# Attention and one output product of a hybrid encoder layer: fillers placed at the ends of heads, gate weights split in two halves, transposed x copied before it is cast

## The chip, the cores and the metric

The kernel runs on one core of a Trainium2 chip. The metric is the device time of one execution in microseconds (us). The engines are TensorE (PE in the profile, with its weight loads as PEld), VectorE (DVE), ScalarE (ACT), GpSimd (POOL) and SyncE (SP), which issues the transfers.

## The reference

One encoder layer on x of 1024 tokens by 1024 channels, in fp32:

```python
h = x @ w_in                                   # 1024 x 5120
qa, ka, va, qb, kb, vb, ga, gb = split(h)      # 6 x 512 columns, 2 x 1024
y_a = chunk_band_attention(qa, ka, va, rel_bias) @ w_proj_a
y_b = stick_breaking_attention(qb, kb, vb) @ w_proj_b
mix = (sigmoid(ga + b_a) * y_a + sigmoid(gb + b_b) * y_b) @ w_out
x = layer_norm(2 ** 0.25 * x + mix)
g, u = split(x @ w_ffn_in)                     # 2 x 2816 columns
x = layer_norm(2 ** 0.25 * x + (silu(g) * u) @ w_ffn_out)
```

Branch A has 8 heads of softmax attention over a band of 9 chunks of 64 keys, with a bias by relative distance. Branch B has 8 heads of stick-breaking attention: the weight of a key is sigmoid(z) times the product of 1 - sigmoid over the keys between it and the query, for all earlier keys.

## The kernel before, in words

**Precision.** A product in fp32 is made of three matmuls on rounded operands, high by high, high by low and low by high. `split` (L109 to L111) makes the two operands: ScalarE casts the high part (L110), VectorE subtracts it from the source (L111). Most large products use seven block products instead of eight, on sums of blocks.

**Stages.** The input projection takes the first 333 us of the profiled execution; the 16 heads of attention run from there to some 650 us; then the projection of branch B and the output product with w_out follow, to some 770; then the FFN's first product (L180) to 1160 and its second (L1496) to the end. The framework's scheduler orders the instructions of each engine from the order of the code and their dependences; some are pinned in the written order (`tc.keep_in_program_order`).

**Attention.** The loop around L1003 goes through 16 heads (`hidx` 0 to 7 are branch A, `br` 0; 8 to 15 are branch B), each in 12 steps (`pos`): 8 for the query group g = 0 and 4 for g = 1. A step contains

- the *weight units* that come due, by the table `LEAD` (L37): one unit makes the scores of 128 queries (L695, L696) and turns them into weights, for branch A in `soft_block` (L729: bias and minimum on VectorE at L738, exp on ScalarE at L744, division on POOL at L749), for branch B in `stick_block` (L763: two sigmoids on ScalarE at L776 and L777, a scan on VectorE at L779, a product on POOL at L784);
- `turn`: PE transposes weights (L807) into a bank "tr", and `split` makes the tile `pt` of it;
- `mult`: the products with the values (L820, L821) into the bank "pv", two steps later (`LAG`); the group's last one is followed by a ScalarE copy (L839) that empties the bank into `yt` or `yv`; a transfer moves one half to other partitions, and POOL adds it in (L843);
- *fillers*: independent matmuls, drawn from the generator `fill_all` (L856) by `fill_until(goal)` (L951). One filler is one 128x128 by 128x512 matmul: of a gate (`gate`, L591, matmuls at L598) or, later, of the projection of branch A (`yAps`). `FILL` (L39) is the number per head; `goal` rises by a twelfth of it in each step, half of it filled ahead of the step's product and half behind. All heads together have 480.

The weights of gates 11 to 15 are prepared while the gate before is in its second half: `begin_w` (L538) loads 128x1024, `end` casts the high part on ScalarE in one instruction (L549) and subtracts on POOL in one (L550).

PSUM has eight banks of 128x512 (L45): "mm" 2 for fillers, "sc" 2 for scores, "tr" 3 for transposes, "pv" 1. In branch B one "tr" bank holds an identity for the scan (`ident_ps`).

**The output product and x.** For token tiles 4 to 7 the product with w_out is made plainly, in two column halves `hf`, tile after tile (24 matmuls each at L117, L118 and L120, tiles `ops4_0` to `ops7_1`). Meanwhile the layer norm of tiles 0 to 3 ends. `x1_operands(0, ...)` (L1171) transposes them on PE (L1178), for each `kt` of 0 to 3 the column blocks kt and kt + 4 into one "tr" bank each (`x1ps0_0` to `x1ps0_7`, four transposes per bank). Out of a bank come a cast and a subtraction (`split`, tiles `x1A1`) and an unrounded copy on ScalarE (L1188, tile `x1raw`); the second call, `x1_operands(1, ...)`, does the same for tiles 4 to 7 with `x1low`. The first call comes once, in the second column half behind tile 4:

```python
            if hf == 1:
                norm_1(tt)
                if tt == 4:
                    x1_operands(0, acc_t)
        if hf == 0:
            left_f(2)
```

The functions that the change touches are these:

## Time and profile before

| | |
|---|---|
| runs shown | 1425.95 us median of 3 (1424.87 to 1426.73) |
| profiled execution | 1425.8 us |
| its span | 1424.0 us, 1.8 us less than its time |
| granted TensorE clock | 0.999 |
| attention, branch A, 333 to 455 us | busy in 122.0 us: PE 120.9, ACT 97.2, DVE 93.4, POOL 66.0 |
| attention, branch B, 455 to 650 us | busy in 195.0 us: PE 193.9, DVE 159.8, ACT 151.4, POOL 138.7 |
| the first call of x1_operands and its surroundings, 751 to 770 us | busy in 19.0 us: PE 18.1, DVE 17.1, ACT 8.4 |

A row of the timeline shows the start in us from the span's start, the duration, the engine, the line, the operation with its tiles (buffer numbers left out), the shapes and the number of like instructions in a row; in brackets stands how long the engine stood idle before it, and what released it. Matmuls are pipelined: a row's duration reaches into the next one's, so a PE that stands in short waits can still count as busy. The profile gives one execution, on the one core.

### The profile page before, as it was taken

What the parts mean: (1) busy time and instruction counts of PE and PEld (TensorE: products, weight loads), DVE (VectorE), ACT (ScalarE), POOL (GpSimd) and SP (SyncE); (2) the same over time, 40 slices, a digit from 0 to 9 for tenths busy, and PEclk for the clock granted to TensorE, in tenths of its full rate; (3) what the DMA queues carried; (4) which work ended last, traced back from release to release, by engine and by line L of the source; (5) the groups of instructions that cost most, each with busy time, mean ns of one, the idle gap of its engine ahead of it and who ended that gap; (6) DMA issues with size and microseconds to landing.
All of it is one profiled execution on the core that took longest, in us unless ns stands there. A gap on an engine that the chain in (4) does not pass through costs nothing.

```text
span 1424.0 us, 19039 instructions
## 1 busy us (share of the span) xinstructions
PE 1412.3 (99%) x6672; PEld 1172.8 (82%) x6672; DVE 1054.5 (74%) x1669; ACT 683.0 (48%) x1188; POOL 245.9 (17%) x313
## 2 busy tenths in 40 slices
PE   9999999999999999999999999999999999999997
PEld 7888888888888888888888888888888888888886
DVE  8866657635777778878988947776777656978767
ACT  6444444555778788774423624444444433212201
POOL 0000000002555779750001000000000000100014
PEclk9999999999999999999999999999999999999999
DMA  7486478856676468755651224443444458787602
GB/s 255 159 295 223 163 251 311 294 183 212 213 222 199 135 228 296 249 196 198 231 198 69 74 75 163 148 148 135 150 159 163 148 192 280 281 312 238 204 15 104
DMA packets 104974, 276.54 MB, mean 194 GB/s; under 512 B 10400, under 2 KB 26784, under 8 KB 104880
## 3 DMA queue, kind: packets, MB, share of 16 engines
q1 hardware_dynamic: 104880, 275.35, 55.9%
q8 instruction: 52, 0.85, 0.3%
q14 instruction: 42, 0.34, 0.1%
HBM read 179.33 MB, written 92.30 MB: 191 GB/s over the span
## 4 chain that ended last, share of the span: by engine, by line
PE 93%; DVE 4%; ACT 2%; issue 1%; DMA 0%; POOL 0%; DVEq 0%; ACTq 0%; SPq 0%
PE sxf L180 16%; PE sxp L180 9%; PE szf L180 8%; PE dx L1496 6%; PE v L482 5%; PE szp L180 5%; PE gps L598 4%; PE syf L180 4%; PE dz L1496 3%; PE yAps L896 3%; PE syp L180 2%; PE tp_b L807 2%; PE ops L1343 2%; PE tp_a L807 2%; PE plain L348 2%; PE fpswh_h L118 2%
## 5 line engine op out<-in xcount | busy, mean ns | idle before, releaser
L784 POOL TENSOR_TENSOR w_b<-w_b,kp_b 128x511 f32<-128x511 f32 (+3 forms) x96 | 96.1, 1017 | 24.9 <-DVE kp_b L779 17.1
L1452 POOL TENSOR_TENSOR wdyt<-wdyt 128x512 f32<-128x512 f32 x8 | 11.2, 1405 | 512.5 <-DVE wdgt L1451 492.0
L779 DVE TENSOR_TENSOR_SCAN kp_b<-kp_b,ident_ps 128x512 f32<-128x512 f32 (+2 forms) x64 | 56.5, 884 | 23.3 <-ACT kp_b L776 22.4
L776 ACT ACTIVATE kp_b<-sc_b 128x512 f32<-128x512 f32 (+3 forms) x96 | 48.4, 505 | 30.7 <-PE sc_b L696 27.4
L180 PE MATMUL szf<-x1S63h,wcf 128*128 128x512 f32 x168 | 55.1, 389 | 0.0
L111 DVE TENSOR_TENSOR pt_b<-tp_b,pt_b 128x512 fp32r<-128x512 f32 (+1 forms) x96 | 50.0, 544 | 6.9 <-ACT pt_b L110 6.3
L719 POOL MEMSET bias<- 64x64 f32 x2 | 0.3, 144 | 313.4 <-ACT bias L715 313.4
L1427 DVE TENSOR_TENSOR x<-dx,x 128x512 f32<-128x512 f32 x64 | 43.3, 685 | 14.7 <-PE dx L1496 14.6
L111 DVE TENSOR_TENSOR sl<-h,sl 128x512 fp32r<-128x512 f32 x56 | 38.3, 685 | 19.5 <-ACT sl L110 19.5
L749 POOL TENSOR_SCALAR w_a<-w_a,st_a 128x640 f32<-128x640 f32 (+2 forms) x64 | 42.3, 666 | 57.3 <-PE sc_a L696 23.8
L110 ACT CAST sl<-h 128x512 fp32r<-128x512 f32 x56 | 34.7, 619 | 35.3 <-PE syf L180 17.1
L110 ACT CAST pt_b<-tp_b 128x512 fp32r<-128x512 f32 (+1 forms) x96 | 47.5, 505 | 8.0 <-PE tp_b L807 7.6
L744 ACT ACTIVATE w_a<-w_a,st_a 128x640 f32<-128x640 f32 (+2 forms) x64 | 44.8, 702 | 13.5 <-DVE st_a L738 12.2
L1156 POOL TENSOR_TENSOR mv<-mv,neghalf 128x1 f32<-128x1 f32 x16 | 11.9, 744 | 222.1 <-DVE mv L1155 222.0
L1274 ACT ACTIVATE h<-sxf 128x512 f32<-128x512 f32 x21 | 12.5, 597 | 77.3 <-PE sxf L180 77.3
L777 ACT ACTIVATE w_b<-sc_b 128x511 f32<-128x511 f32 (+3 forms) x96 | 48.6, 506 | 0.0
L111 DVE TENSOR_TENSOR pt_a<-tp_a,pt_a 128x512 fp32r<-128x512 f32 (+1 forms) x96 | 44.9, 485 | 4.8 <-ACT pt_a L110 3.1
L807 PE MATMUL tp_b<-ident,w_b 128*128 128x128 f32 x288 | 47.8, 273 | 0.4 <-DVE pt_b L111 0.3
L110 ACT CAST pt_a<-tp_a 128x512 fp32r<-128x512 f32 (+1 forms) x96 | 39.1, 432 | 11.0 <-PE tp_a L807 10.8
L807 PE MATMUL tp_a<-ident,w_a 128*128 128x128 f32 x240 | 43.2, 275 | 1.0 <-POOL w_a L749 0.4
L807 PEld LDWEIGHTS tp_b<-ident,w_b 128*128 128x128 f32 x288 | 35.6, 140 | 9.6 <-PE sc_b L696 1.3
L598 PE MATMUL gps<-xl,wh_g 128*128 128x512 f32 x96 | 43.0, 448 | 0.0
(1787 smaller groups left out, 4814.3 us busy)
## 6 DMA issues: line engine op xcount, KB each, us to landing
s_dr<-sl SPq DMA_DIRECT2D x112, 256.0 KB, 2.3
sd<-s_dr SPq DMA_DIRECT2D x56, 512.0 KB, 4.7
wLf<-in_w_ffn_in_dram SPq DMA_DIRECT2D x22, 512.0 KB, 4.5
wRf<-in_w_ffn_in_dram SPq DMA_DIRECT2D x22, 512.0 KB, 3.6
v_dr<-vc SPq DMA_DIRECT2D x16, 512.0 KB, 3.2
qs<-q_dr SPq DMA_DIRECT2D x16, 512.0 KB, 6.9
kh<-k_dr SPq DMA_DIRECT2D x16, 512.0 KB, 6.1
kl<-k_dr SPq DMA_DIRECT2D x16, 512.0 KB, 6.9
```

What stands on the lines that cost most here:

```text
L110: return (nc.scalar.copy(dst_h, src), nc.vector.tensor_tensor(dst_l, src, dst_h.bitcast(F32), ALU.subtract))
L111: nc.vector.tensor_tensor(dst_l, src, dst_h.bitcast(F32), ALU.subtract))
L180: mm(acc, lw[:, ks], rx, start=(first and kt == i == 0), stop=(kt == 3 and i == 2), skip_group_check=not first)
L482: mm(accs[j], a, b, start=(first and kt == n == 0), stop=(kt == 3 and n == 2), skip_group_check=True)
L598: mm(acc[hf], lw[:, ks], rx[k][:, (LO, HI)[hf]], start=(k == j == 0), stop=(k == KT - 1 and j == 2))
L744: nc.scalar.activation(s[:, 0:w], s[:, 0:w], AF.Exp, bias=st[:, m:m + 1], scale=-1.0, accum_out=st[:, 2:3])
L776: nc.scalar.activation(kp[:, c0:e], sc[:, 0:n], AF.Sigmoid, scale=-1.0)
L777: nc.scalar.activation(be[:, m0:e], sc[:, m0 - c0:n], AF.Sigmoid)
L779: nc.vector.tensor_tensor_scan(kp[:, 0:e], kp[:, 0:e], ident_ps()[:, 0:e], 0.0, ALU.mult, ALU.add)
L784: nc.gpsimd.tensor_tensor(be[:, m0:e], be[:, m0:e], kp[:, m0 - 1:e - 1], ALU.mult)
L807: tr(tp[:, (qb - lo_q) * P:(qb - lo_q + 1) * P], wt[qb - q0][:, (kb - qb) * P:(kb - qb + 1) * P], ident)
L1496: mm(acc, a, b, start=(first and i == n == 0), stop=(i == n - 1 == 1), skip_group_check=not first)
```

## The change

There are three parts. Line numbers behind the first places shift by up to 22 in the changed kernel: L598 becomes L607, L695 L706, L749 L760, L807 L818, L820 L831, L1188 L1207.

**Fillers.** `FILL` of heads 8 to 11 goes from 40, 40, 39, 39 to 39, 39, 38, 38. In the loop, ahead of a step's weight units: in head 7 `goal` rises by 2 more at pos 3 and again at pos 4, and at pos 5 it falls by 1 (three more in all); in the other heads of branch A it rises by 1 at pos 3 and falls by 1 at pos 5. In branch A at pos 2 `fill_until(goal + 0.5)` is called ahead of the step's weight units, which at that step hold the first scores of the next head.

**Gate weights.** Inside `fill_all`, `end` casts and subtracts columns 0 to 511 where it did all 1024, and puts columns 512 to 1023 on the list `rest`; `gate` takes them from it behind the third of eight blocks of its second half, nine fillers later.

**Transposed x.** `x1_operands` copies each bank to SBUF first, and `split` reads the copy; this holds for both calls. The first call is made in three pieces: block 0 behind the whole first column half, blocks 1 and 2 behind tile 4 of the second, block 3 behind tile 5.

```diff
-FILL = (18, 18, 18, 18, 18, 18, 18, 34, 40, 40, 39, 39, 40, 38, 38, 38)
+FILL = (18, 18, 18, 18, 18, 18, 18, 34, 39, 39, 38, 38, 40, 38, 38, 38)
...
-        def end(tied=False):
+        def end(tied=False, rest=None):
             hi = hl(f"wh_{name}", F32R)
             lo = hl(f"wl_{name}", F32R)
-            for ins in (nc.scalar.copy(hi, r),
-                        lo_eng.tensor_tensor(lo, r, hi.bitcast(F32), ALU.subtract)):
-                if tied:
-                    tc.keep_in_program_order(ins)
+
+            def part(cs):
+                for ins in (nc.scalar.copy(hi[:, cs], r[:, cs]),
+                            lo_eng.tensor_tensor(lo[:, cs], r[:, cs], hi[:, cs].bitcast(F32),
+                                                 ALU.subtract)):
+                    if tied:
+                        tc.keep_in_program_order(ins)
+
+            if rest is None:
+                part(slice(0, 1024))
+            else:
+                part(LO)
+                rest.append(lambda: part(HI))
             return hi, lo
...
                 for k in range(KT):
                     yield from part(hf, k)
+                    if hf and k == 2 and rest:
+                        rest.pop()()
                 take(hf)
...
-            yield from gate(i, w, lambda: got.append(end(True)))
+            yield from gate(i, w, lambda: got.append(end(True, rest)))
...
+        if hidx == 7 and pos in (3, 4):
+            goal += 2
+        elif hd["br"] == 0 and pos in (3, 5):
+            goal += 4 - pos
+        if hd["br"] == 0 and pos == 2:
+            fill_until(goal + 0.5)
         while wi < min(hidx * 8 + LEAD[hd["br"]][pos], len(wunits)):
...
-    def x1_operands(hf, acc_t):
+    def x1_operands(hf, acc_t, kts=range(4)):
...
-                    split(o[:, LO], o[:, HI], tps[i])
-                    nc.scalar.copy(raw[:, (LO, HI)[i]], tps[i])
+                    part = raw[:, (LO, HI)[i]]
+                    nc.scalar.copy(part, tps[i])
+                    split(o[:, LO], o[:, HI], part)
...
-                if tt == 4:
-                    x1_operands(0, acc_t)
+                if tt < 6:
+                    x1_operands(0, acc_t, ((1, 2), (3,))[tt - 4])
         if hf == 0:
             left_f(2)
+            x1_operands(0, acc_t, (0,))
```

PE at the change from head 2 to head 3 of branch A, before: the last product of head 2 (`pv_a2_1`), the first scores of head 4 (`sc_a4`), transposes of head 3's weights (`tp_a3`), fillers of gate 11 (`gps11`), and the first product of head 3 (`pv_a3_0`).

```order
L821 MATMUL pv_a2_1_3478<-pt_a2_1_4_3474,v2_3100 128x128
L695 MATMUL sc_a4_0_0_3536<-kh4_3405,qs4_3403 128x320
L696 MATMUL sc_a4_0_0_3536<-kl4_3407,qs4_3403 128x320
L695 MATMUL sc_a4_0_1_3540<-kh4_3405,qs4_3403 128x320
L696 MATMUL sc_a4_0_1_3540<-kl4_3407,qs4_3403 128x320
L807 MATMUL tp_a3_0_6_3547<-ident_69,w_a3_0_2_3296 128x128
L807 MATMUL tp_a3_0_6_3547<-ident_69,w_a3_0_3_3297 128x128
L598 MATMUL gps11_0_3322<-xh5_255,wl_g11_3001 128x512
L598 MATMUL gps11_0_3322<-xh6_257,wh_g11_3000 128x512
L807 MATMUL tp_a3_0_7_3555<-ident_69,w_a3_0_3_3297 128x128
L598 MATMUL gps11_0_3322<-xl6_258,wh_g11_3000 128x512
L820 MATMUL pv_a3_0_3561<-pt_a3_0_4_3496,v3_3335 128x512
```

The same place in the changed kernel, between the last product of head 2 (one row above) and the first of head 3:

```order
L607 MATMUL gps11_0_3324<-xh5_255,wl_g11_3001 128x512
L706 MATMUL sc_a4_0_0_3539<-kh4_3407,qs4_3405 128x320
L707 MATMUL sc_a4_0_0_3539<-kl4_3409,qs4_3405 128x320
L706 MATMUL sc_a4_0_1_3543<-kh4_3407,qs4_3405 128x320
L707 MATMUL sc_a4_0_1_3543<-kl4_3409,qs4_3405 128x320
L818 MATMUL tp_a3_0_6_3550<-ident_69,w_a3_0_2_3299 128x128
L818 MATMUL tp_a3_0_6_3550<-ident_69,w_a3_0_3_3300 128x128
L607 MATMUL gps11_0_3324<-xh6_257,wh_g11_3000 128x512
L818 MATMUL tp_a3_0_7_3557<-ident_69,w_a3_0_3_3300 128x128
L607 MATMUL gps11_0_3324<-xl6_258,wh_g11_3000 128x512
L607 MATMUL gps11_0_3324<-xh6_257,wl_g11_3001 128x512
L831 MATMUL pv_a3_0_3564<-pt_a3_0_4_3498,v3_3338 128x512
```

One filler moved ahead of the first scores, and a later filler moved ahead of the first product; behind that product one filler fewer stands after the next group of transposes.

ScalarE at the first call of `x1_operands`, before, with what each instruction waits for in brackets; `x1A10_0` is the rounded operand of block 0, `x1A11_0` that of block 4, `x1raw0` the copy of both:

```order
L110 CAST x1A10_0_7827<-x1ps0_0_7816 128x512 [waits PE_49]
L110 CAST x1A11_0_7831<-x1ps0_4_7821 128x512 [waits PE_49]
L110 CAST x1A10_1_7846<-x1ps0_1_7835 128x512 [waits PE_49]
L1188 COPY x1raw0_7826<-x1ps0_0_7816 128x512 [waits DVE_49]
L110 CAST x1A11_1_7850<-x1ps0_5_7840 128x512 [waits PE_49]
L1188 COPY x1raw0_7826<-x1ps0_4_7821 128x512 [waits DVE_49]
L1188 COPY x1raw1_7845<-x1ps0_1_7835 128x512 [waits DVE_49]
```

ScalarE at the first call in the changed kernel, block 0 and then the beginning of block 1:

```order
L1207 COPY x1raw0_7800<-x1ps0_0_7790 128x512 [waits PE_49]
L1207 COPY x1raw0_7800<-x1ps0_4_7795 128x512 [waits PE_49]
L110 CAST x1A10_0_7801<-x1raw0_7800 128x512 [waits Activation_49]
L110 CAST x1A11_0_7805<-x1raw0_7800 128x512 [waits Activation_49]
L1207 COPY x1raw1_7855<-x1ps0_1_7845 128x512 [waits PE_49]
L1207 COPY x1raw1_7855<-x1ps0_5_7850 128x512 [waits PE_49]
L110 CAST x1A10_1_7856<-x1raw1_7855 128x512 [waits Activation_49]
```

The copies stand ahead of the casts and wait for PE alone; the casts read the copy and wait for it on their own engine.

POOL while PE multiplies head 3 and the weights of head 4 are made, before, where the weights of gate 12 are subtracted (`wl_g12`), between divisions of head 4's weights (`w_a4`) and the addition of head 3's result (`yt1`):

```order
L749 TENSOR_SCALAR w_a4_0_1_3532<-w_a4_0_1_3532,st_a4_1_3568 128x640
L550 TENSOR_TENSOR wl_g12_3627<-wr_g12_3319,wh_g12_3626 128x1024
L749 TENSOR_SCALAR w_a4_0_2_3533<-w_a4_0_2_3533,st_a4_2_3603 128x640
L749 TENSOR_SCALAR w_a4_0_3_3534<-w_a4_0_3_3534,st_a4_3_3647 128x640
L749 TENSOR_SCALAR w_a4_1_0_3684<-w_a4_1_0_3684,st_a4_4_3686 128x512
L843 TENSOR_TENSOR yt1_3437<-yt1_3437,yv_a3_0_3673 64x512
```

The same place in the changed kernel:

```order
L760 TENSOR_SCALAR w_a4_0_1_3535<-w_a4_0_1_3535,st_a4_1_3571 128x640
L552 TENSOR_TENSOR wl_g12_3629<-wr_g12_3321,wh_g12_3628 128x512
L760 TENSOR_SCALAR w_a4_0_2_3536<-w_a4_0_2_3536,st_a4_2_3605 128x640
L760 TENSOR_SCALAR w_a4_0_3_3537<-w_a4_0_3_3537,st_a4_3_3649 128x640
L760 TENSOR_SCALAR w_a4_1_0_3686<-w_a4_1_0_3686,st_a4_4_3688 128x512
L854 TENSOR_TENSOR yt1_3439<-yt1_3439,yv_a3_0_3675 64x512
L552 TENSOR_TENSOR wl_g12_3629<-wr_g12_3321,wh_g12_3628 128x512
```

The subtraction stands in its old place at half the size, and its second half comes behind three divisions and the addition.

More of the change, by code (lines that the diff above doesn't have):

```diff
@@ L853, in value_steps @@
         return steps
+    rest = []
     def fill_all():
```

7 lines of the change are left out of this document (4 added, 3 removed).

## The prediction

> **What bounds the kernel now.** I read the page first, then who TensorE (PE) waited for, then the timeline in four places.
>
> ```profile
> span 1424.0 us, 19039 instructions
> ...
> PE 1412.3 (99%) x6672; PEld 1172.8 (82%) x6672; DVE 1054.5 (74%) x1669; ACT 683.0 (48%) x1188; POOL 245.9 (17%) x313
> ```
>
> PE is busy for 99% of the span, so whatever this change gains must be time in which PE stands still; it removes no matmul. The view of waits names little of that:
>
> ```profile
> PE x1ps L1178 <- ACT x1raw L1188: 0.9, 1, 0.9
> PE tp_a L807 <- POOL w_a L749: 0.4, 1, 0.4
> PE tp_a L807 <- DVE pt_a L111: 0.4, 1, 0.4
> ```
>
> Busy time hides the rest, because one matmul's row overlaps the next one's. So I read starts instead. In a stretch where nothing waits:
>
> ```profile
> 724.64 0.39 PE L117 MATMUL ops<-wh_o,mo 128*128 128x512 f32 x1
> ...
> 751.39 0.39 PE L118 MATMUL ops<-wl_o,mo 128*128 128x512 f32 x1
> ```
>
> These are the first and the last of 119 rows: 26.75 us over 118 steps is 0.227 us from start to start of a 512-column matmul, though each row says 0.39. That 0.227 is also the price of one filler. A longer step is a wait, or the change between transposes and matmuls, which the change mostly leaves alone.
>
> **Transposed x.** This is the largest single wait.
>
> ```profile
> 751.86 1.47 PE L1178 MATMUL x1ps<-ident,acc 128*128 128x128 f32 x12
> ...
> 754.33 0.40 PE L120 MATMUL ops<-wh_o,mo 128*128 128x512 f32 x1
> 755.59 0.66 PE L1178 MATMUL x1ps<-ident,acc 128*128 128x128 f32 x4 [0.87 <-ACT x1raw L1188]
> 756.00 0.49 PE L117 MATMUL ops<-wh_o,mo 128*128 128x512 f32 x1
> 756.33 0.40 PE L118 MATMUL ops<-wl_o,mo 128*128 128x512 f32 x1
> ```
> ```profile
> 752.49 1.57 ACT L110 CAST x1A<-x1ps 128x512 fp32r<-128x512 f32 x3 [4.03 <-PE x1ps L1178]
> 754.95 0.58 ACT L1188 COPY x1raw<-x1ps 128x512 f32<-128x512 f32 x1 [0.90 <-DVE x1A L111]
> ```
>
> The matmul at 754.33 is followed after 1.26 us instead of 0.23: 1.03 us lost. Twelve transposes (1.22 us to the next matmul, 0.10 each) fill the three transpose banks; the fourth bank's need waits until the copy ends at 755.53, and that copy had waited for VectorE's subtraction, since cast, subtraction and copy all read the bank in turn. In the changed order the copy stands first and waits for PE alone; cast and subtraction read the copy. Block 0 goes ahead of the second loop, where both its banks are free for 24 matmuls. The tight place is then the group of blocks 1 and 2: four banks' worth with three banks, so its fourth (x1ps0_6) needs the copy of x1ps0_1. From the rows: the cast began 752.49 - 751.86 = 0.63 us after the first transpose, a copy takes 0.58, PE followed the copy's end by 0.06, so the bank is free after 1.27 us, and PE asks for it after 12 x 0.10 to 0.11 = 1.2 to 1.3 us. I count no wait there. Each change from transposes to matmuls makes the second matmul 0.33 - 0.23 = 0.10 us late, and the changed order has 6 such changes instead of 9; with what the first one gains by starting early I count 0.06 each, 0.2 together. Other small waits in the second half stay. Sum **1.2 us**, from 0.8 (a tight bank costs 0.2 twice) to 1.5.
>
> **First scores and first value product.** One filler per softmax head moves ahead of the next head's first scores, and a second ahead of a group's first product, with one taken out behind it; up to that product PE has one filler more.
>
> ```profile
> 374.06 0.47 PE L598 MATMUL gps<-xl,wh_g 128*128 128x512 f32 x1
> 374.52 0.50 PE L820 MATMUL pv_a<-pt_a,v 128*128 128x512 f32 x1
> ...
> 404.32 0.28 PE L821 MATMUL pv_a<-pt_a,v 128*128 128x128 f32 x1
> 404.51 0.41 PE L695 MATMUL sc_a<-kh,qs 128*128 128x320 f32 x1
> ...
> 405.34 0.48 PE L598 MATMUL gps<-xh,wl_g 128*128 128x512 f32 x1
> 405.66 0.39 PE L598 MATMUL gps<-xh,wh_g 128*128 128x512 f32 x1
> ...
> 405.92 0.47 PE L598 MATMUL gps<-xl,wh_g 128*128 128x512 f32 x1
> 406.38 0.50 PE L820 MATMUL pv_a<-pt_a,v 128*128 128x512 f32 x1
> ...
> 437.64 0.48 PE L598 MATMUL gps<-xl,wh_g 128*128 128x512 f32 x1
> 438.11 0.50 PE L820 MATMUL pv_a<-pt_a,v 128*128 128x512 f32 x1
> ```
> ```profile
> 405.75 0.58 ACT L839 COPY yv_a<-pv_a 128x512 f32<-128x512 f32 x1
> ```
>
> A filler behind a transpose steps 0.32 us (405.34 to 405.66); ahead of the product it steps 0.46, so the product waits 0.14, until ScalarE's copy (ending 406.33) has emptied the only product bank. The first score starts 0.19 us after a 128-column matmul that needs some 0.10: another 0.09. Together 0.23, one filler. The copy hangs on the last scores of the head before, which come ahead of the moved filler, so it isn't made later; the filler fills the wait. The place repeats in six heads (374.52 and 438.11 have steps of 0.46 and 0.47; 358.90, below, has more, but one filler is all that is put there). 6 x 0.22 = **1.3 us**, from 0.4 (the copy moves along) to 1.4. What is late next: the step from which a filler was taken has transposes and products whose inputs were made a filler earlier, so nothing.
>
> **Gate weights in two pieces.** The cast on ScalarE and the subtraction on GpSimd (POOL) stand in front of softmax work.
>
> ```profile
> 398.38 2.39 POOL L550 TENSOR_TENSOR wl_g<-wr_g,wh_g 128x1024 fp32r<-128x1024 f32 x1
> ```
> ```profile
> 358.90 0.50 PE L820 MATMUL pv_a<-pt_a,v 128*128 128x512 f32 x1 [0.17 <-ACT yt L839]
> ...
> 401.47 0.49 PE L807 MATMUL tp_a<-ident,w_a 128*128 128x128 f32 x3
> 402.39 0.33 PE L807 MATMUL tp_a<-ident,w_a 128*128 128x128 f32 x1 [0.42 <-POOL w_a L749]
> ```
> ```profile
> 354.81 1.06 ACT L549 CAST wh_g<-wr_g 128x1024 fp32r<-128x1024 f32 x1
> ...
> 446.87 0.57 ACT L839 COPY yt<-pv_a 128x512 f32<-128x512 f32 x1
> ```
>
> Gate 12: the fourth transpose comes 0.92 us after three that take 0.33, 0.59 lost, since the divisions on POOL queued behind 2.39 us. Half of it, 1.2, ends that soon enough: 0.6. Gate 11: the cast at 354.81 delays all of ScalarE's queue; half of it gives back some 0.5, of which the 0.17 idle at 358.90 and a little before it count beyond the filler: 0.25. Against that, gate 13's second cast now stands directly ahead of the copy at 446.87 and pushes it and two casts behind it by 0.6; I charge 0.25. Sum **0.6 us**, from -0.6 (five second pieces at 0.25 each against the two gains, halved) to 0.9.
>
> [...]
>
> ```profile
> L549 ACT CAST wh_g<-wr_g x6: 1048/1059/1105, 318.0 to 499.3; 128x1024 fp32r<-128x1024 f32 x6
> ```
> ```profile
> L110 ACT CAST sl<-h x56: 604/621/625, 842.2 to 1150.3; 128x512 fp32r<-128x512 f32 x56
> ```
> ```profile
> L110 ACT CAST x1A<-x1ps x16: 586/594/674, 752.5 to 786.4; 128x512 fp32r<-128x512 f32 x16
> ```
>
> [...]
>
> **Change of branches.** Head 7 gets 3 fillers more, heads 8 to 11 one fewer each.
>
> ```profile
> 453.50 1.28 ACT L776 ACT_TABLE_LOAD   x1
> ```
> ```profile
> 456.39 0.39 PE L598 MATMUL gps<-xh,wl_g 128*128 128x512 f32 x1
> 456.91 0.50 PE L695 MATMUL sc_b<-kh,qs 128*128 128x512 f32 x1
> ...
> 457.61 0.39 PE L598 MATMUL gps<-xh,wh_g 128*128 128x512 f32 x1
> 458.41 0.66 PE L807 MATMUL tp_a<-ident,w_a 128*128 128x128 f32 x4 [0.41 <-DVE pt_a L111]
> ```
>
> Steps of 0.52 and 0.80 where 0.23 would do: 0.29 + 0.57 = 0.86 us, both hanging on the table load through the first sigmoids and scans, which fillers don't shift. By the order PE does two fillers more before 458.41, and one 256-column product less (0.12): 0.33 us filled, and one more filler fills about 0.1 later: **0.4 us**, from 0 to 0.8. Taking four fillers from heads 8 to 11 could open waits there of up to 4 x 0.227 = 0.9; the waits view lists next to none in that stretch, so I take 0.2.
>
> **Sum.** 1.2 + 1.3 + 0.6 + 0.4 - 0.2 = 3.3 us. The profiled execution took 1425.8 (span 1424.0 and 1.8 around it), against a median of 1425.95; 1425.8 - 3.3 = 1422.5.
>
> **Rivals.** (1) *The waits only move.* ScalarE's and VectorE's queues follow PE's pace, and the products wait as long behind more fillers: the 1.3 and 0.4 are lost and the 0.2 stays: 1425.8 - 1.2 - 0.6 + 0.2 = 1424.2. For it: both waits end on other engines. Against: the copy's inputs precede the moved fillers. [...] (3) *Hidden waits go too* (steps of 0.1 to 0.2 in head 0 and behind gate 12's second group): 1421.2. (4) *Slower*: the second pieces land ahead of the copies that empty the only product bank, in all five gates. A copy pushed by 0.62, with the casts behind it, costs 0.62 and again 0.62 when the transposes behind it come late: 5 x 1.24 = 6.2, less 3.3 + 0.25 already charged: 1425.8 - 3.55 + 6.2 = 1428.5. It decides from 0.7 us a gate on; only gate 13 shows the piece in that place, so it is unlikely. That the order isn't what the change says is excluded: the rows stand.
>
> **How the numbers follow.** Forecast 0.53, rival 1 0.22, rival 2 0.1, rival 3 0.1, rival 4 0.05. A measurement tells 0.2% from no change, 2.85 us, so faster means below 1423.1. Forecast and rival 3 lie below, but the forecast's bounds cross the line: of 0.63 I leave 0.57 faster; the rest is same, but for 0.05 slower. The range takes in both middle rivals and the upper sums: 1420.5 to 1424.8.
>
> **What would show it.** Step by step: no idle time before x1ps in the waits view; steps of 0.32 instead of 0.46 before pv_a; 402.39's wait gone; the wait before tp_a at the table load down by 0.3. Wrong would be waits named pv_a <- ACT yt near gate 13, or new idle time in heads 8 to 11.

## The result and the profile after

The changed kernel takes 1420.72 us (median of 7 runs, 1420.49 to 1421.86) against 1424.93 for the kernel before in the same set (median of 7, 1424.87 to 1426.73): a ratio of the runs of 0.9966 with a 95% interval of 0.9956 to 0.9975, that is 3.6 to 6.3 us faster (the two medians differ by 4.2). The forecast was 1422.5, 3.3 us faster than the profiled execution; the two profiled executions differ by 1425.8 - 1420.72 = 5.1. The direction was right and the sum was too small; most of the places were right too, and the section on why says which were not. The head of the changed kernel's page:

```profile
span 1418.9 us, 19024 instructions
...
PE 1408.4 (99%) x6672; PEld 1171.9 (83%) x6672; DVE 1054.6 (74%) x1669; ACT 683.9 (48%) x1193; POOL 246.8 (17%) x318
```

The same 6672 matmuls, and 3.9 us less of PE's busy time: as the prediction had it, waits stood inside the busy rows. ScalarE has five instructions more (the five second casts) and 0.9 us more busy time. What PE still waits for, by the view of waits:

```profile
PE tp_b L818 <- DVE pt_b L111: 0.6, 2, 0.3
PE tp_a L818 <- DVE pt_a L111: 0.3, 1, 0.3
PE tp_a L818 <- POOL w_a L760: 0.2, 1, 0.2
...
PE sc_b L706 <- ACT w_b L788: 0.2, 1, 0.2
```

The wait of transposed x for its copy is gone from the list. Its rows now (timeline of PE, then of ScalarE, where the copy of block 0 is the first of two):

```profile
742.22 1.03 PE L1197 MATMUL x1ps<-ident,acc 128*128 128x128 f32 x8
743.01 0.48 PE L117 MATMUL ops<-wh_o,mo 128*128 128x512 f32 x1
...
748.55 1.93 PE L1197 MATMUL x1ps<-ident,acc 128*128 128x128 f32 x16
```
```profile
744.26 1.07 ACT L1207 COPY x1raw<-x1ps 128x512 f32<-128x512 f32 x2
745.23 1.15 ACT L110 CAST x1A<-x1raw 128x512 fp32r<-128x512 f32 x2
749.19 1.08 ACT L1207 COPY x1raw<-x1ps 128x512 f32<-128x512 f32 x2 [2.81 <-PE x1ps L1197]
```

Block 0's eight transposes begin as a group, and their copies are late (744.26, behind three weight casts) without harm, because 24 matmuls follow. Blocks 1 and 2, sixteen transposes on three banks, run through without a bracket: the place that the prediction called tight holds.

The change of heads, the counterpart of the rows from 404.32 to 406.38 in the prediction:

```profile
401.80 0.22 PE L831 MATMUL pv_a<-pt_a,v 128*128 128x128 f32 x1
401.85 0.28 PE L832 MATMUL pv_a<-pt_a,v 128*128 128x128 f32 x1
401.96 0.45 PE L607 MATMUL gps<-xh,wl_g 128*128 128x512 f32 x1
402.25 0.31 PE L706 MATMUL sc_a<-kh,qs 128*128 128x320 f32 x1
...
402.98 0.48 PE L607 MATMUL gps<-xh,wh_g 128*128 128x512 f32 x1
403.30 0.27 PE L818 MATMUL tp_a<-ident,w_a 128*128 128x128 f32 x1
403.32 0.48 PE L607 MATMUL gps<-xl,wh_g 128*128 128x512 f32 x1
403.64 0.40 PE L607 MATMUL gps<-xh,wl_g 128*128 128x512 f32 x1
403.92 0.50 PE L831 MATMUL pv_a<-pt_a,v 128*128 128x512 f32 x1
404.25 0.39 PE L832 MATMUL pv_a<-pt_a,v 128*128 128x512 f32 x1
```

From the last product of one head to the first of the next it takes 403.92 - 401.85 = 2.07 us with four fillers, where it took 406.38 - 404.32 = 2.06 with three. One filler, 0.23 us, is done there at no cost, as forecast. That is not all that the place gains, as the next table shows.

To read where time goes, the starts of each group's first products on PE were compared between two traces. A start that comes earlier counts as gained, and since the kernels have done more or fewer fillers by then, each filler more or less counts 0.227 us. The rows go from one head's first product of group 1 to the next head's; before the first of them these executions differ by -1.4 to 0.4 us, nearly all of it in the input projection, whose code all of them share. Each column is one execution.

```
us gained against the kernel before, by the traces
                           changed  heads  gates  branch  no branch
                                    e1     e2     e3      edit, e7
head 0 to 1 (gate 11)       0.90    0.55   0.58    0.02     0.88
head 1 to 2                 0.37    0.38   0.16   -0.03     0.38
head 2 to 3                 0.58    0.43   0.35    0.01     0.58
head 3 to 4 (gate 12)       0.52    0.10   0.69   -0.12     0.90
head 4 to 5                 0.82    0.79   0.27   -0.01     0.82
head 5 to 6                 0.55    0.17  -0.04    0.01     0.55
change of branches          0.50   -0.34   0.04    0.64    -0.11
heads 8 to 15              -0.39    0.00  -0.33   -0.53    -0.38
sum                         3.85    2.08   1.72   -0.01     3.62
```

With 1.2 us behind attention (the lead grows from 4.22 us at the first `yBps` to 5.39 at the first `plainhl_0f`) and 0.4 ahead of the first row, less 0.3 lost again at 796 us, that is the 5.1 us between the two spans. The 0.4 is a difference between executions and not the change's work.

The 0.3 is a new wait. Before, the first product into `syf` (a sum of the FFN) follows the one ahead of it after 0.23 us:

```profile
800.92 0.39 PE L118 MATMUL plainhl_512f<-x1A,wlf0h 128*128 128x512 f32 x1
801.15 0.62 PE L180 MATMUL syf<-x1A,wlf2h 128*128 128x512 f32 x2
```

In the changed kernel one matmul into `sxf` has come in between, and the first product into `syf` starts 0.49 us after it, released by VectorE:

```profile
795.95 0.39 PE L180 MATMUL sxf<-x1S63h,wbf1h 128*128 128x512 f32 x1
796.44 0.30 PEld L180 LDWEIGHTS syf<-x1A,wlf2h 128*128 128x128 f32 x2 [0.52 <-DVE h L1268]
```

All seven kernels here that copy x before they cast it have this step, 0.46 to 0.49 us, and none of the other nine has it.

### The profile page after: what moved, and what is told of

Read it like the earlier page. It is cut to its first block, busy times and chain, and to the rows that moved or that the text cites. A ratio compares the mean times of both kernels' runs of the same rounds, so it can differ in the third digit from the quotient of the medians.

```text
span 1418.9 us, 19024 instructions
## 1 busy us (share of the span) xinstructions
PE 1408.4 (99%) x6672; PEld 1171.9 (83%) x6672; DVE 1054.6 (74%) x1669; ACT 683.9 (48%) x1193; POOL 246.8 (17%) x318
## 4 chain that ended last, share of the span: by engine, by line
PE 95%; DVE 2%; ACT 1%; issue 1%; DMA 0%; POOL 0%; DVEq 0%; ACTq 0%; POOLq 0%
PE sxf L180 16%; PE sxp L180 9%; PE szf L180 8%; PE dx L1518 6%; PE v L482 5%; PE szp L180 5%; PE gps L607 4%; PE syf L180 4%; PE dz L1518 3%; PE yAps L909 3%; PE ops L1364 3%; PE syp L180 2%; PE tp_b L818 2%; PE tp_a L818 2%; PE plain L348 2%; PE fpswh_h L120 2%
## 5 line engine op out<-in xcount | busy, mean ns | idle before, releaser
L760 POOL TENSOR_SCALAR w_a<-w_a,st_a 128x640 f32<-128x640 f32 (+2 forms) x64 | 42.2, 668 | 48.7 <-PE sc_a L707 27.3
L818 PE MATMUL tp_b<-ident,w_b 128*128 128x128 f32 x288 | 47.6, 273 | 0.8 <-DVE pt_b L111 0.6
L818 PE MATMUL tp_a<-ident,w_a 128*128 128x128 f32 x240 | 43.1, 275 | 0.6 <-DVE pt_a L111 0.3
L818 PEld LDWEIGHTS tp_b<-ident,w_b 128*128 128x128 f32 x288 | 35.4, 140 | 10.0 <-DVE pt_b L111 1.6
L607 PE MATMUL gps<-xl,wh_g 128*128 128x512 f32 x96 | 42.5, 443 | 0.0
```

The source lines that it names most:

```text
L607: mm(acc[hf], lw[:, ks], rx[k][:, (LO, HI)[hf]], start=(k == j == 0), stop=(k == KT - 1 and j == 2))
L818: tr(tp[:, (qb - lo_q) * P:(qb - lo_q + 1) * P], wt[qb - q0][:, (kb - qb) * P:(kb - qb + 1) * P], ident)
```

## The experiments

**The four parts one by one.** Each kernel is the kernel before with one part of the change.

Fillers of heads 0 to 6:

```diff
+        if hd["br"] == 0 and hidx < 7 and pos in (3, 5):
+            goal += 4 - pos
+        if hd["br"] == 0 and pos == 2:
+            fill_until(goal + 0.5)
```

> Fillers of heads 0 to 6 alone (one ahead of the next head's first scores, one ahead of a group's first product, one taken out behind), all else as before. Theory: each of the six places gains 0.40 us, 0.23 for the filler that fills the wait and 0.17 because the second product (128x384) behind the group-1 start no longer waits; 6 x 0.40 and some 0.1 around: 2.5 us faster than before. Rival 1: the place gains only the filler, 0.23, and the 0.17 belongs to the halved gate weights: 1.4 us. Rival 2: the waits move with the fillers: 0 to 0.3 us.

Measured: 1423.82 us against 1426.20, ratio 0.9983 (0.9974 to 0.9991). In the table the sum from head 0 to 6 is 2.42 us, and the places without gate weights (head 1 to 2, head 2 to 3) give 0.38 and 0.43. The theory's 0.40 holds there; the other places give 0.10 to 0.79, and that the six sum to the theory's 2.4 is partly luck. Where the other 0.17 comes from shows on PE behind the group-1 product (the first product of a head's group g = 1). The kernel before:

```profile
369.13 0.40 PE L821 MATMUL pv_a<-pt_a,v 128*128 128x512 f32 x1
369.36 0.33 PE L820 MATMUL pv_a<-pt_a,v 128*128 128x384 f32 x1
369.61 0.19 PEld L821 LDWEIGHTS pv_a<-pt_a,v 128*128 128x128 f32 x1 [0.29 <-DVE pt_a L111]
369.61 0.44 PE L821 MATMUL pv_a<-pt_a,v 128*128 128x384 f32 x1
369.89 0.34 PE L695 MATMUL sc_a<-kh,qs 128*128 128x384 f32 x1
```

The kernel with the fillers alone, at the same place:

```profile
369.96 0.39 PE L821 MATMUL pv_a<-pt_a,v 128*128 128x512 f32 x1
370.19 0.34 PE L820 MATMUL pv_a<-pt_a,v 128*128 128x384 f32 x1
370.36 0.34 PE L821 MATMUL pv_a<-pt_a,v 128*128 128x384 f32 x1
370.54 0.34 PE L695 MATMUL sc_a<-kh,qs 128*128 128x384 f32 x1
```

Steps of 0.25 and 0.28 become 0.17 and 0.18. Before, the second 384-column product waited for VectorE's subtraction into `pt_a`, its operand, and the matmul behind it came 0.1 late as well; PE's rows overlap and carry no bracket, but the row of its weight load (PEld) does. The same two steps are 0.16 to 0.19 us too long in heads 1, 2 and 5 of the kernel before; in head 4 this place loses 0.44, in head 0 the second step 0.1, in heads 3 and 6 nothing. With the fillers alone, and in the changed kernel, nothing is lost there in heads 0 to 5. Nothing was edited at this place, and PE comes to it with the same number of fillers done. But ScalarE, no longer held up at the change of heads, is ahead: its copy of the group before starts 1.21 us ahead of the group-1 product (368.52 and 369.73), where it was 0.87 (368.02 and 368.89).

Gate weights in two halves (the diff of `begin_w`, `gate` and `fill_all` shown above, nothing else):

> Gate weights in two halves alone, all else as before. Theory: 0.6 us at gate 12's division, 0.3 at gate 11's cast, and a cost of up to 0.25 at gate 13: 0.6 to 0.9 us faster. Rival 1: the halves also remove the 0.17 us wait of the second product in six heads: 1.6 to 1.9 us faster. Rival 2 (second halves in front of the copies cost what the first ones give): within 0.2 us of before.

Measured: 1424.60 against 1426.20, ratio 0.9988 (0.9979 to 0.9997). 1.6 us by the times, 1.72 by the trace. The size is rival 1's and the cause is not: the wait behind the group-1 product goes in head 1 alone, shrinks from 0.44 to 0.17 us in head 4, and stays in heads 2 and 5. The theory left out two gains and priced gate 11 too low. One is 0.33 us ahead of head 3's group-1 product: before, a product of 128 columns starts 0.34 us after the one ahead of it (397.72 to 398.06), with these halves 0.06, and its operand is made on ScalarE behind gate 12's cast at 395.37. The other is the 0.27 in head 4; the expectations below call it gate 13, but gate 13's cast comes only in head 6 (438.69 before). The charge for gate 13 did come: 0.2 us are lost in head 6 of this kernel, and 0.33 in the changed one, where the second cast stands directly ahead of the copy:

```profile
442.70 0.60 ACT L551 CAST wh_g<-wr_g 128x512 fp32r<-128x512 f32 x1
443.21 0.58 ACT L850 COPY yt<-pv_a 128x512 f32<-128x512 f32 x1
444.42 0.33 PE L831 MATMUL pv_a<-pt_a,v 128*128 128x384 f32 x1
444.81 0.45 PE L832 MATMUL pv_a<-pt_a,v 128*128 128x384 f32 x1
```

In the changed kernel that loss stands in the table's row of the change of branches.

Change of branches:

```diff
-FILL = (18, 18, 18, 18, 18, 18, 18, 34, 40, 40, 39, 39, 40, 38, 38, 38)
+FILL = (18, 18, 18, 18, 18, 18, 18, 34, 39, 39, 38, 38, 40, 38, 38, 38)
...
+        if hidx == 7 and pos in (3, 4):
+            goal += 2
+        elif hidx == 7 and pos == 5:
+            goal -= 1
```

> Three fillers more in head 7 (two ahead of its pos 3, two ahead of pos 4, one fewer at pos 5) and one fewer each in heads 8 to 11 alone. Theory: 0.7 to 0.9 us gained by the first products of head 8, some 0.4 lost in heads 11 and later where a filler is missing: 0.4 us faster in all. Rival: no loss later, 0.8 us faster. Other rival: the waits at the table load stay as they are and only move: 0 or slightly slower.

Measured: 1426.07 against 1426.20, ratio 1.0001 (0.9992 to 1.0010). By the trace 0.64 us gained at the change of branches and 0.53 lost in the heads behind. The loss is larger than the theory's 0.4, and alone the edit is worth nothing that can be seen.

Transposed x (the diff of `x1_operands` and of its calls shown above, nothing else):

> Copy first and the three pieces of the first call of x1_operands alone. Theory (the forecast's 1.2 us): the wait of 1.03 us before the transposes is gone and nothing takes its place ahead of the FFN's first product: 1.0 to 1.2 us faster. Rival: the casts, now behind the copies, come late for the first matmuls on the rounded operands, and half of it is given back: 0.5 us.

Measured: 1425.07 against 1426.20, ratio 0.9992 (0.9983 to 1.0000): 1.1 us, and by the trace the lead grows from 0.28 us at the first `yBps` to 1.41 at the first `plainhl_0f`, 1.13. The theory holds up to there, ahead of the FFN's first product. Behind it the new wait at `syf` takes 0.3 back, and 0.8 is left at the end. The rival expected half to be given back for casts that come late; a quarter to a third is, and what releases the late product is VectorE's `h`, not a cast.

By the times the four parts alone sum to 2.4 + 1.6 + 0.1 + 1.1 = 5.2 us, and the whole brings 3.6 to 6.3. By the table the parts don't add up place by place: from head 4 to 5 they give 0.79 + 0.27 and the whole 0.82, from head 5 to 6 they give 0.13 and the whole 0.55. That the sums agree is partly luck.

**The two fillers at a change of heads, apart.** Kernel before plus the lines for pos 2 alone, and kernel before plus the lines for pos 3 and 5 alone.

> Only the filler ahead of the next head's first scores (at pos 2 of heads 0 to 7); nothing moves ahead of the first product. Each place is read in the trace, from the group-1 product of one head to the first product of the next. Theory: the scores' wait of 0.09 us and the 0.1 of the matmul behind it go, but the product then has one filler less behind the scores and waits longer: 0 to 0.1 us per head, since the copy that empties the bank is what ends the stretch. Rival: the two waits are independent, the filler ahead of the scores brings 0.2 us a head by itself, and the first product keeps its 0.14.

One execution, 1424.78 us. The kernel before, run beside this and the other single executions, took 1424.6 to 1427.6, so single executions are read by the trace here. By the trace 0.01, -0.01, -0.02, 0.00 and 0.02 us are gained in the five places without gate 12. From head 3 to 4 it shows 0.58, for there a wait is missing that comes and goes between executions (below). As the theory says, the filler ahead of the scores alone gains nothing: the copy ends the stretch (in the kernel before it ends at 406.33 and the product starts at 406.38).

> Only the other half of the filler edit in heads 0 to 6: one filler more by pos 3, ahead of the group's first product, one fewer at pos 5; nothing is moved ahead of the first scores. Per head, read in the trace from the first product of one head to that of the next. Theory: the filler ahead of the product fills the copy's wait, 0.23 us, and the wait of the second group's products goes too, 0.17: 0.40 a head, as with both; the filler ahead of the scores is worth 0 to 0.1 more. Rival: the two are needed together, and this one alone brings 0.1 to 0.2 a head.

1424.42 us in one execution, by the trace 0.35, 0.05, 0.43, -0.22, 0.65 and 0.16 from head 0 to 6, together 1.42 where both fillers give 2.42. The theory falls and the rival's reading holds in kind: nothing plus 1.4 makes 2.4, so the two need each other. With the product's filler alone a new wait comes up in front of the next scores:

```profile
379.48 0.31 PE L696 MATMUL sc_a<-kl,qs 128*128 128x320 f32 x1
380.00 0.41 PE L695 MATMUL sc_a<-kh,qs 128*128 128x320 f32 x1 [0.21 <-DVE st_a L738]
```

This is the place from which the filler was taken, and 0.52 us lies between two scores instead of 0.15. The prediction said that there nothing would be late. With both fillers the same place loses 0.15 (380.95 to 381.14 and on to 381.39 in e1's trace) and gets 0.12 back before the next group-1 product.

**Size or place of the gate weights.** Cast and subtraction whole, both at the later place:

```diff
-                part(LO)
-                rest.append(lambda: part(HI))
+                rest.append(lambda: part(slice(0, 1024)))
```

> Gate weights in one piece as before, but cast and subtraction both nine fillers later (where the change puts the second half); nothing else changed. Theory (it is the size: a long instruction blocks its queue wherever it stands): the waits at gate 11 (0.42 and 0.28 us) and gate 12 (0.59 and 0.28) vanish from their places, and waits of like size, 0.4 to 0.6 us each, come up where the whole pieces now stand: no gain in sum, within 0.4 us of before. Rival (it is the place): 1.2 us or more faster, as with the halves.

1423.97 us in one execution; by the trace 1.51 us from head 0 to 6, where the halves give 2.01, and 1.21 in all, where they give 1.72. The theory (size) falls. A wait of the expected kind does come up where the whole pieces stand, one of them 0.31 us at gate 12,

```profile
405.20 0.50 PE L830 MATMUL pv_a<-pt_a,v 128*128 128x512 f32 x1 [0.31 <-ACT yv_a L849]
```

but the move alone keeps some two thirds of the gain. Most of what the halves bring, they bring because at least half of the work leaves a bad place.

**Which engine's halves.** Subtraction in halves with the cast whole in its old place, and cast in halves with the subtraction whole behind the second one:

```diff
-                part(LO)
-                rest.append(lambda: part(HI))
+                tc.keep_in_program_order(nc.scalar.copy(hi, r))
+                low(LO)
+                rest.append(lambda: low(HI))
```

> Only GpSimd's subtraction of the gate weights in two halves, the second nine fillers later; ScalarE's cast whole in its old place. Theory: GpSimd's part is gate 12's division alone, 0.4 to 0.6 us, and the rest of the halves' 1.7 to 2.0 us by the trace (gate 11 0.4 and 0.3, gate 12 0.3 at its products, gate 13 0.3) is ScalarE's: this kernel gains 0.4 to 0.7. Rival: GpSimd's queue is what delays the softmax in all gates: 1.5 us or more here.

1425.08 us in one execution. By the trace 0.60 us, all of it from head 3 to 4; elsewhere -0.03 to 0.03. GpSimd's part is gate 12's division, as the theory says. The row that changes (GpSimd, the subtraction and the two divisions behind it):

```profile
398.43 1.29 POOL L559 TENSOR_TENSOR wl_g<-wr_g,wh_g 128x512 fp32r<-128x512 f32 x1
399.70 1.59 POOL L766 TENSOR_SCALAR w_a<-w_a,st_a 128x640 f32<-128x640 f32 x2
```

```diff
-                part(LO)
-                rest.append(lambda: part(HI))
+                high(LO)
+                rest.append(later_part)    # high(HI), then the whole subtraction
```

> The counterpart of the run on the subtraction: ScalarE's cast of the gate weights in two halves, the second nine fillers later with GpSimd's whole subtraction right behind it. Theory: ScalarE's queue accounts for what the subtraction's halves left, by the trace 0.4 and 0.3 us around gate 11, 0.3 at gate 12's products and 0.3 at gate 13: 1.2 to 1.5 us gained from the first group-1 product to the first product of head 6, less a new wait of some 0.3 us where the whole subtraction stands at gate 12 now. Rival: the whole subtraction, wherever it stands, costs its 0.6 us at gate 12 and ScalarE's halves bring 0.7 us or less.

1424.54 us in one execution. By the trace 0.58 us from head 0 to 1, -0.34 from 1 to 2, then 0.33, 0.71 and 0.24: 1.49 from head 0 to 6. Gate 12's division no longer waits, since the whole subtraction now stands behind it; without the 0.6 that e11 shows for this place and with the -0.34 put aside ScalarE's halves give some 1.2 us, as the theory has it. The -0.34 is the new wait, but at gate 11 and not at gate 12:

```profile
370.50 0.33 PE L826 MATMUL tp_a<-ident,w_a 128*128 128x128 f32 x1 [0.30 <-POOL w_a L768]
```

So the gate term is some two thirds ScalarE's and one third GpSimd's, one execution each, and GpSimd's third only where gate 12's wait is there at all (next). The prediction had it the other way round.

**Gate 12's wait is not in every execution.** In the traces of kernels with the same code at that place it is there or not. What goes with it is the start of GpSimd's addition of head 2's second result, counted from a product of head 3 on PE (the second one of 512 columns in group 0):

```
subtraction whole        addition starts after    wait at gate 12's division
before                       1.75 us                  0.59 us
heads (e1)                   1.92                     0.67
branch (e3)                  1.89                     0.67
first product (e9)           2.08                     0.67
copy only (e10)              1.82                     0.65
x (e4)                       1.24                     0.10
first scores (e5)            1.16                     none
subtraction halved
changed                      2.46                     0.35
subtraction halves (e11)     1.73                     none
fill late (e8)               1.70                     none
two fillers more (e14)       1.67                     none
no branch (e7)               1.25                     none
gates (e2)                   1.12                     none
```

The addition waits for a transfer, and the subtraction and the divisions queue behind it. Whole, the subtraction left no wait behind a start at 1.16 us and 0.10 behind one at 1.24; halved, none up to 1.73. From 1.75 with the whole piece (0.59) to 1.73 with the half (none) is the cleanest pair. Two executions, the changed kernel's and one that differs behind this place only:

```profile
394.99 1.28 POOL L854 TENSOR_TENSOR yt<-yt,yv_a 64x512 f32<-64x512 f32 x1 [3.63 <-DMA yv_a<-yt]
396.26 0.79 POOL L760 TENSOR_SCALAR w_a<-w_a,st_a 128x640 f32<-128x640 f32 x1
397.02 1.29 POOL L552 TENSOR_TENSOR wl_g<-wr_g,wh_g 128x512 fp32r<-128x512 f32 x1
```
```profile
394.63 1.28 POOL L854 TENSOR_TENSOR yt<-yt,yv_a 64x512 f32<-64x512 f32 x1 [2.41 <-DVE pt_a L111]
```

GpSimd stood idle for 3.63 us in the one and 2.41 in the other before the same addition. That the landing of the transfer makes the difference is what the first row names; it is not shown by a run, and what delays the landing was not tried.

An addition one step later was meant to take it out of the way:

```diff
-                        later.append([3 + hd["br"], add])
+                        later.append([4, add])
```

> The changed kernel with the addition of a head's result on GpSimd (yt plus yv, which waits for a transfer) one step later in branch A. In the traces so far the wait at gate 12's division is 0.59, 0.67, 0.67, 0.10 and 0 us in kernels that have the same code there, and each time GpSimd stood idle for 2.6 to 3.3 us ahead of that addition. Theory: the transfer's landing, in front of GpSimd's queue, sets that wait; with the addition a step later GpSimd's idle time in front of it is gone in most heads and the wait of 0.35 us that the changed kernel's profile shows there goes: 0 to 0.4 us faster than the changed kernel. Rival: the later addition collides with the second half's subtraction or with the next head's divisions: 0.2 to 1 us slower.

1420.80 us, ratio to before 0.9968 (0.9956 to 0.9980), the same as the changed kernel. Its trace has no wait at gate 12 and is 0.38 us ahead there, but the kernels e7 and e8, with the addition in its old place, are too, and GpSimd's idle time in front of additions is still up to 3.07 us. The theory's mechanism is not tested by it: the two cases can't be told apart.

**Is the branch edit worth anything?** The changed kernel without it:

```diff
-        if hidx == 7 and pos in (3, 4):
-            goal += 2
-        elif hd["br"] == 0 and pos in (3, 5):
+        if hd["br"] == 0 and hidx < 7 and pos in (3, 5):
```

> The changed kernel without its edit at the change of branches (head 7 and heads 8 to 11 with the fillers of before), heads 0 to 6, gate halves and x kept. Theory, from the edits by themselves: the edit gains some 0.5 us at the first products of head 8 and loses as much in heads 11 and 12, so this kernel takes the time of the changed one, within 0.3 us. Rival 1: with the other edits PE reaches the table load earlier and waits there longer, the edit is worth 0.7 us or more, and this kernel is slower than the changed one by that. Rival 2: it is faster than the changed one by 0.4 us, since only the losses go.

1421.80 us against 1426.14, ratio 0.9969 (0.9958 to 0.9981), which is not told apart from the changed kernel by the times. By the trace, rival 1 in kind: -0.11 at the change of branches where the changed kernel has 0.50, so the edit is worth 0.6 there. The kernel with the fillers of heads 0 to 6 alone shows the same, -0.34. That PE comes earlier there and waits longer at the table load (1.28 us on ScalarE in the kernel before and in the changed one) is the author's reading of the table; no row of these two kernels shows it. The heads behind lose 0.39 us with the edit and 0.38 without it, so in the sum the missing fillers cost nothing more here. But the places differ: without the edit head 11 alone loses (0.36), with it heads 11 and 12. With it a wait that the prediction named as a sign of being wrong is there:

```profile
540.48 0.66 PE L818 MATMUL tp_b<-ident,w_b 128*128 128x128 f32 x4 [0.30 <-DVE pt_b L111]
```

The fillers taken from later heads:

```diff
-FILL = (18, 18, 18, 18, 18, 18, 18, 34, 39, 39, 38, 38, 40, 38, 38, 38)
+FILL = (18, 18, 18, 18, 18, 18, 18, 34, 40, 40, 39, 39, 39, 37, 37, 37)
```

> The changed kernel with the fillers for head 7 taken from heads 12 to 15 (39, 37, 37, 37) and heads 8 to 11 left at 40, 40, 39, 39. Theory: the waits that the changed kernel has in heads 11 and 12 (0.30 and 0.15 us idle before transposes) come from the missing fillers and go, and like ones come in heads 13 to 15, where two waits of 0.3 stand already: 0 to 0.3 us faster than the changed kernel. Rival: those waits stay, because PE arrives earlier whatever fills it: same time as the changed kernel within 0.1 us in the trace.

1421.60, ratio 0.9967 (0.9955 to 0.9979). By the trace it loses 0.32 us more than the changed kernel in heads 8 to 15: waits stand now at 541.89, 595.88 and 617.88 (0.39, 0.32 and 0.33 us idle). The wait at 541.89 stays although heads 10 and 11 have their fillers back, as the rival says, and a new one comes in head 13. Neither forecast the loss: in this execution the kernel with fillers missing late loses more than the one with fillers missing early.

Two more fillers at the table load:

```diff
-FILL = (18, 18, 18, 18, 18, 18, 18, 34, 39, 39, 38, 38, 40, 38, 38, 38)
+FILL = (18, 18, 18, 18, 18, 18, 18, 34, 38, 38, 38, 38, 40, 38, 38, 38)
...
         if hidx == 7 and pos in (3, 4):
-            goal += 2
+            goal += 3
```

> The changed kernel with two more fillers in head 7 (three instead of two at pos 3 and at pos 4), taken from heads 8 and 9 (38 each). Theory: the waits at the table load (0.16 and 0.29 us idle in the changed kernel's profile) shrink by one filler each, 0.3 to 0.45 us, and heads 8 and 9, where the trace shows no wait, give the fillers up for nothing: 0.3 us faster than the changed kernel. Rival: as in the run with fillers taken from heads 12 to 15, what is gained comes back as waits in the heads with fewer fillers: within 0.1 us or slower.

1421.09, ratio 0.9968 (0.9956 to 0.9980): no gain. In the changed kernel PE has these rows,

```profile
453.11 0.50 PE L706 MATMUL sc_b<-kh,qs 128*128 128x512 f32 x1 [0.16 <-ACT w_b L788]
...
454.60 0.66 PE L818 MATMUL tp_a<-ident,w_a 128*128 128x128 f32 x4 [0.29 <-DVE pt_a L111]
```

and in the one with two more fillers these:

```profile
453.09 0.50 PE L706 MATMUL sc_b<-kh,qs 128*128 128x512 f32 x1
...
454.58 0.66 PE L818 MATMUL tp_a<-ident,w_a 128*128 128x128 f32 x4 [0.53 <-DVE pt_a L111]
```

One filler fills the first wait; the transposes start at the same time, 454.6, and their wait grows from 0.29 to 0.53. Between the scores and the transposes one filler fewer is left, so that up to there both kernels have done the same, and the rest stands behind. The transposes hang on the table load's chain, as the other rival of e3 had it (in the changed kernel: the load at 449.70, 1.28 us; VectorE idle for 1.84 us until the first sigmoid; scans at 451.62 and 452.95; the subtraction into `pt_a` at 454.15): here fillers move the wait and don't shorten it. In the heads behind, 0.15 us is lost.

**Order or pieces of transposed x.** Copy first, with the call in one piece as before:

> Transposed x copied before it is cast, but the first call of x1_operands in one piece behind tile 4 as before. Theory: the copies wait for PE alone, so of the 1.03 us ahead of the fourth bank about half is left, since twelve transposes still ask for three banks in a row and a fourth one 1.2 us after the first, when the first copy ends 1.2 to 1.3 after it: 0.9 to 1.1 us faster than before by the trace from 751 to 772 us. Rival: without the pieces the fourth bank still waits for most of the time, 0.3 us or less gained, and the pieces are what counts.

1425.75 us in one execution, which shows no gain by itself (the kernel before beside it: 1425.69). By the trace the lead grows from -0.22 us at the first `x1ps` to 0.73 at `plainhl_0f`: 0.95, the size of the theory, of the 1.13 with the pieces. Behind it 0.4 is lost again, as in the other kernels with the copy first. The order of the copies is five sixths of this part. The theory left half of the wait ahead of the fourth bank; none is left, for PE has

```profile
752.07 2.42 PE L1178 MATMUL x1ps<-ident,acc 128*128 128x128 f32 x20
```

twenty transposes in a row, 0.11 us each, where twelve went through before.

## Why the prediction was too small, step by step

- **What bounds the kernel: right.** PE does the same 6672 matmuls, and what is gained are steps between their starts that became shorter; the waits view names few of them.
- **Transposed x, 1.2 us: right up to the FFN's first product.** 1.1 by the times, 1.13 by the trace; the tight group of blocks 1 and 2 didn't wait. The forecast stopped there and left out the wait at `syf` behind it, 0.3, which leaves 0.8.
- **First scores and first product, 1.3 us: the mechanism right, the size off.** The filler filled 0.23 as said. Alone the edit gave 2.42 us from head 0 to 6. The step that failed is "together 0.23, one filler": it priced the two waits at the edited place and left out the 384-column products behind the group-1 product, which lost 0.16 to 0.19 us in heads 1, 2 and 5 and 0.44 in head 4, and no longer do once ScalarE and VectorE are ahead. That is rival 3's mechanism (hidden waits go too), which named other places. "What is late next ... so nothing" was wrong for one of the fillers alone (e9's new wait) and nearly right for both (0.15 lost, 0.12 back).
- **Gate weights, 0.6 us: the step that failed most**, 1.6 by the times and 1.72 by the trace alone. Gate 12's division is worth the 0.6 (e11), in executions that have the wait at all. Gate 11 was put at 0.25 and gave 0.58 from head 0 to 1; the cast at gate 12, 0.33, and head 4's wait, 0.27, were not counted. The charge of 0.25 for gate 13 was right: 0.2 alone, 0.33 in the changed kernel. The error was to count idle time in brackets (0.17 at 358.90) for ScalarE's share, where the steps of PE show more.
- **Change of branches, 0.4 less 0.2: near for the edit alone, by chance.** Alone it gains 0.64 and loses 0.53, both more than forecast. With the other parts it is worth 0.6, by the author's reading since without it PE, now earlier, waits longer at the table load; that it depends on the other parts was in no term.
- **The sum.** The parts of attention alone make 2.08 + 1.72 - 0.01 = 3.8 us by the trace, together 3.85, against 2.1 forecast: 1.75 us too little. Transposed x brings 0.3 less than forecast at the end of the span, and 0.4 lies ahead of attention, in code that didn't change; together that is the 1.8 between 3.3 and 5.1.
- **Rivals.** Rival 1 fell with e1: the waits didn't move. Rival 2, that smaller instructions cost ScalarE's time and PE waits for all of it, fell too: ScalarE's busy time grew by 0.9 us (683.0 to 683.9) and the kernel still came out faster than forecast. The ten casts of 128x512 of gate weights take 0.631 us on average where one of 128x1024 took 1.066, 2 x 0.631 - 1.066 = 0.20 us more per gate. The casts of x take a median of 0.632 to 0.656 us from SBUF (rows below; in ns, minimum, median and maximum) where it was 0.594 from PSUM (the last of the three rows of casts in the prediction), 0.038 to 0.062 us more. No run prices either for the kernel by itself. Rival 4 came at gate 13 alone: a step of 0.39 instead of 0.17 us stands behind its second piece (`pv_a` at 444.42, the next at 444.81) and 0.11 behind that, 0.33 where the rival says 1.24. Rival 3's 1421.2 was the nearest.

```profile
L110 ACT CAST x1A<-x1raw x8: 632/632/656, 745.2 to 757.9; 128x512 fp32r<-128x512 f32 x8
L110 ACT CAST x1A<-x1low x8: 629/656/684, 774.6 to 781.2; 128x512 fp32r<-128x512 f32 x8
```

- **The signs that it named.** No idle time is left before `x1ps`, and the step before `pv_a` is 0.28 where 0.46 stood. The wait of 402.39 is not gone in this execution (0.35 of 0.59 left), and the one before `tp_a` at the table load is down by 0.12, not by 0.3. New idle time came in head 11, and near gate 13 a loss without a bracket: of the signs of being wrong one came, and one came half.
- **What stays open.** Why the heads behind the change of branches lose 0.4 us in the changed kernel, with and without the branch edit; whether the wait at `syf` can be had away by keeping `sxf` behind it, which was not tried; and what makes the transfer ahead of GpSimd's addition land later in some executions.

## What to carry to other kernels

Where the bottleneck engine shows 99% busy, take the step from start to start and count every step that is too long, those just behind an edited place above all: here the stretch that stopped holding up the helper engines also freed products that no one had touched (0.16 to 0.19 us in each of heads 1, 2 and 5). Here the long preparing instructions (1.06 us on ScalarE, 2.39 on GpSimd) were worth moving away from short work in their queues first and cutting second (1.2 us by the move alone, 1.7 by the halves, by the trace of one execution each). And gate 12's wait, 0.59 to 0.67 us in five executions of the same code and 0.10 or none in two, is a price with a chance: look for such a wait in several traces before it goes into a sum.

## What the runs showed of the hardware

- GpSimd's subtraction of 128x1024 takes 2.39 us (kernel before) and one of 128x512 1.29 (changed kernel): cutting it in two adds 0.19 us of work.
- A matmul of 512 columns behind one that had waited starts 0.33 to 0.34 us after it instead of 0.23 (406.38 to 406.72 before, and 403.92 to 404.25 in the changed kernel, where the wait was only 0.05): in these rows a short wait costs some 0.1 more than its own length. The forecast counted it for transposes only.
- The same wait in the same code was 0.59 to 0.67 us in five executions and 0.10 or none in two (the table of gate 12).
